# One fused hybrid decoder layer: the order of each engine's instructions made with the scheduler's detailed model of queues and semaphores

## The chip, the cores and the metric

The kernel runs on one core of one Trainium2 chip. A core has a matmul engine (TensorE, PE in the profile, with its weight loads as PEld), VectorE (DVE), ScalarE (ACT), GpSimd (POOL, nearly unused here) and SyncE (SP), which only issues DMAs here. Each engine takes its instructions in the order of its own queue and waits at an instruction until the semaphores it names have come. The metric is the device time of one execution in microseconds; the figure for a kernel is the median of three runs.

## The reference

One layer of a decoder trunk on a sequence of 2048 tokens with 1024 features, in float32. Three token mixers read the same normalised input through one projection, their outputs are joined and projected back, and a gated term is added:

```python
def hybrid_layer(x, p_i, pre_norm_w, w_in, ...):
    hn = rms_norm(x, pre_norm_w)
    u = jnp.einsum('bld,de->ble', hn, w_in)
    z, xbc, dt_raw, conf_in, conf_gate, q, k, v, attn_gate = split_columns(u)
    y_ssd = ssd_mixer(z, xbc, dt_raw, ssd_conv_w, ssd_conv_b, ...)
    y_conf = conformer_conv(conf_in, conf_dw_w, conf_dw_b, ...) * jax.nn.silu(conf_gate)
    y_attn = sliding_window_attention(q, k, v, attn_sinks, rel_bias) * jax.nn.silu(attn_gate)
    y = jnp.concatenate([y_ssd, y_conf, y_attn], axis=-1)
    h = x + rms_norm(jnp.einsum('ble,ed->bld', y, w_out), post_norm_w)
    gate = jax.nn.sigmoid(jnp.einsum('bld,de->ble', h, ple_gate))
    return h + jnp.einsum('blp,pd->bld', p_i, ple_proj) * gate
```

`ssd_mixer` is a state-space mixer with 16 heads in chunks of 128 tokens: within a chunk a masked product, between chunks a state that each chunk updates. `conformer_conv` is a causal convolution over 31 taps with a layer norm. `sliding_window_attention` has 8 heads on 2 key heads and looks back 128 tokens. `depth` is 1.

## The kernel before

The sequence is cut into four chunks of 512 tokens. Every large product is made of three matmuls on operands that are split into a high and a low part: hi·lo, lo·hi and hi·hi. `split` makes the parts, the high one on ACT (L190) and the low one on DVE (L191). A matmul of this kind has 512 columns; the projection has 4032 of them (L443, L444, L445), the output projection 1536 (L1048 to L1050), and the gate stage the rest (L207 to L209). They are the bulk of PE's work.

**Stage 1** makes the projection `w_in` and the three mixers, in two halves of two chunks. At the start chunk 0 is projected while the norm of its rows is still being made. For chunk 1 the order is fixed by data: `rsqrt_cols` (L142 to L151) gives rstd as columns, a transpose on PE (L175) turns them into a row, ACT copies it (L177) and writes it out by a DMA from its own queue (L179), SP loads it back to all partitions (L186), DVE weighs the chunk with it (L433, in `pre_apply`), and `split` gives the operands `ah` and `al`. The evictions of projected tiles (L478) multiply by such a row too (`rb__229` for chunk 0).

After the head a half runs through units: convolution (C), attention (A) and state-space (S) units, in turns. A unit's projection runs through `proj`, and the work behind it is written as generators that stand in the list `pending` and are advanced between groups of matmuls. An SSD unit (`ssd_front`, `ssd_back`) loads `Ab` (L868), transposes its input (L505), forms `xd` (L894) and `xw` (L896), `eA` and `Ab` by ACT (L899 to L904), makes state increments on PE (L910), carries the state `H` on DVE (L918), weighs `eA` and `Ab` on DVE (L927, L928), and multiplies into one PSUM tile `ps_y`: L937 from `Ab`, L940 from `eA` and `H`. A convolution of four taps is L487 on ACT, three L489 and an L492 on DVE. These small matmuls (64 or 128 columns wide, or the transposes) stand between the 512-column ones of the next unit's projection. Of the scratch tiles that hold 1024 columns (`Ab`, `eA`, the attention's `S`, and in stage 2 `ya`, `ysd`, `cvo`) there are four in all; PSUM has five tiles for projections (`ps_pp`), two for small products (`ps_m`) and one `ps_y`.

**Stage 2** multiplies by `w_out`, chunk by chunk. `prep` loads what the mixers wrote (L236: `ya`, `ysd`, `cvo`), norms and splits it. `stats` makes the norms for the next chunk, among them the column sums (L159) of `csum` (L263) and of `ssum`, and two rows through L175. **Stage 3** is the gated term.

The program is written with a tile framework. The kernel's text gives the tiles, the pools with their numbers of buffers, and a sequence of operations; the framework finds which operation needs which, plays the program on a model of the chip, and emits each engine's instructions in the order that the model gives. No priority is written by hand. The text of the kernel sets which work is offered at which time, the model sets what stands ahead of what on each queue, the SP queue and ACT's DMAs among them.

## Time and profile before

| | us |
|---|---|
| three runs | 1840.11, 1841.65, 1845.51 |
| median | 1841.65 |
| the profiled execution | 1850.51 |
| its span, first to last instruction | 1848.7 |
| DMA, mean over the span | 143 GB/s |

The profiled execution was 0.5% longer than the median. The profile's page lists busy time by engine, a chain of waits followed back from the last instruction, and groups of instructions by line. Two more views are used: the waits of one engine, with what they waited for, and stretches of the span with the busy time of each engine. A busy PE contains short gaps between matmuls, since their ends are modelled; distances between starts show those.

### The profile page before, as it was taken

How to read it: one execution, taken by the hardware profiler on the slowest of the kernel's cores; microseconds unless marked ns; L12 is line 12 of the kernel's file. 1: busy time of each engine (PE TensorE's matmuls, PEld its weight loads, DVE VectorE, ACT ScalarE, POOL GpSimd, SP SyncE). 2: the span in 40 equal slices, each digit the busy share in tenths (PEclk: the TensorE clock that was granted, in tenths of full speed). 3: DMA queues.
4: the chain of work that ended last, by engine and by line, in shares of the span. 5: the costliest groups of instructions: out<-in, count | busy, mean ns of one | idle time of the engine just before them, and what ended most of it. 6: DMA issues, size and time to landing. Idle time of an engine off the chain costs nothing.

```text
span 1848.7 us, 25168 instructions
## 1 busy us (share of the span) xinstructions
PE 1810.7 (98%) x9386; PEld 1461.6 (79%) x9386; DVE 1385.1 (75%) x2400; ACT 818.6 (44%) x1565; POOL 0.2 (0%) x4
## 2 busy tenths in 40 slices
PE   6999999999999999999999999999999999999998
PEld 5877787787888778878788887877888788887887
DVE  6859769759869875976975996988777867466543
ACT  5525425524726542542653371465444444343331
POOL 0000000000000000000000000000000000000000
PEclk9999999999999999999999999999999999999999
DMA  7443233224433433333332332346677766578554
GB/s 234 132 133 98 80 102 96 61 78 106 171 112 111 121 102 104 91 87 89 100 115 76 101 99 87 82 145 230 214 242 236 245 228 199 202 240 280 189 188 131
DMA packets 118982, 265.09 MB, mean 143 GB/s; under 512 B 12619, under 2 KB 20428, under 8 KB 118860
## 3 DMA queue, kind: packets, MB, share of 16 engines
q1 hardware_dynamic: 108428, 246.65, 40.9%
q10 hardware_dynamic: 10432, 16.83, 4.1%
q8 instruction: 74, 1.21, 0.3%
q14 instruction: 48, 0.39, 0.1%
HBM read 205.05 MB, written 39.50 MB: 132 GB/s over the span
## 4 chain that ended last, share of the span: by engine, by line
PE 78%; DMA 8%; DVE 6%; ACT 4%; issue 2%; ACTq 1%; SPq 0%; DVEq 0%
PE ps_pp L443 15%; PE ps_pp L444 14%; PE ps_pp L445 14%; PE ps_pp L1048 4%; PE ps_pp L1049 4%; PE ps_pp L1050 4%; PE ps_pp L208 3%; PE ps_pp L209 3%; PE ps_pp L207 3%; PE ps_m L766 2%; PE ps_y L940 2%; PE ps_y L838 2%; DMA Ab<-acs_d 2%; PE ps_y L937 2%; PE ps_m L816 1%
## 5 line engine op out<-in xcount | busy, mean ns | idle before, releaser
L443 PE MATMUL ps_pp<-al,whi 128*128 128x512 f32 x1344 | 536.6, 400 | 13.6 <-DVE al L393 10.4
L444 PE MATMUL ps_pp<-ah,wlo 128*128 128x512 f32 x1344 | 534.5, 398 | 0.0
L445 PE MATMUL ps_pp<-ah,whi 128*128 128x512 f32 x1344 | 534.1, 397 | 0.0
L191 DVE TENSOR_TENSOR wlo<-wst,whi 128x1024 fp32r<-128x1024 f32 x214 | 234.1, 1102 | 179.8 <-ACT whi L190 179.4
L443 PEld LDWEIGHTS ps_pp<-al,whi 128*128 128x128 f32 x1344 | 254.4, 189 | 73.1 <-DVE al L393 10.4
L190 ACT CAST whi<-wst 128x1024 fp32r<-128x1024 f32 x214 | 202.9, 951 | 242.0 <-DMA wst<-in_w_gate_dram 86.1
L691 DVE SCALAR_TENSOR_TENSOR acc<-gl,par_sb,acc 128x1024 f32<-128x1024 f32 x240 | 307.3, 1280 | 2.3
L444 PEld LDWEIGHTS ps_pp<-ah,wlo 128*128 128x128 f32 x1344 | 254.6, 189 | 55.8 <-issue 6.5
L445 PEld LDWEIGHTS ps_pp<-ah,whi 128*128 128x128 f32 x1344 | 254.5, 189 | 54.4 <-issue 4.9
L489 DVE SCALAR_TENSOR_TENSOR cv<-raw,par_sb,cv 128x512 f32<-128x512 f32 x144 | 107.6, 747 | 22.7 <-ACT cv L487 22.0
L208 PE MATMUL ps_pp<-ah,wlo 128*128 128x512 f32 x256 | 100.2, 391 | 3.7 <-DVE wlo L191 3.7
L1048 PE MATMUL ps_pp<-bl,whi 128*128 128x512 f32 x256 | 101.5, 399 | 0.6 <-ACT whi L190 0.6
L1048 PE MATMUL ps_pp<-al,whi 128*128 128x512 f32 x256 | 100.4, 393 | 0.7 <-DVE al L191 0.7
L1049 PE MATMUL ps_pp<-bh,wlo 128*128 128x512 f32 x256 | 101.1, 395 | 0.0
L1050 PE MATMUL ps_pp<-bh,whi 128*128 128x512 f32 x256 | 100.7, 394 | 0.0
L207 PE MATMUL ps_pp<-al,whi 128*128 128x512 f32 x256 | 100.1, 391 | 0.6 <-ACT whi L190 0.5
L1049 PE MATMUL ps_pp<-ah,wlo 128*128 128x512 f32 x256 | 100.1, 391 | 0.0
L1050 PE MATMUL ps_pp<-ah,whi 128*128 128x512 f32 x256 | 100.0, 390 | 0.0
L209 PE MATMUL ps_pp<-ah,whi 128*128 128x512 f32 x256 | 99.7, 389 | 0.0
L796 ACT ACTIVATE S<-S,nm 128x256 f32<-128x256 f32 (+1 forms) x128 | 62.8, 492 | 80.0 <-DVE nm L782 74.6
L903 ACT ACTIVATE Ab<-Ab,acs 128x128 f32<-128x128 f32 x256 | 82.4, 391 | 0.4
L937 PE MATMUL ps_y<-Ab,xd 128*64 128x128 f32 x512 | 61.5, 282 | 2.0 <-issue 2.0
(235 smaller groups left out, 2592.1 us busy)
## 6 DMA issues: line engine op xcount, KB each, us to landing
wst<-in_w_in_dram SPq DMA_DIRECT2D x88, 512.0 KB, 3.5
wst<-in_w_out_dram SPq DMA_DIRECT2D x64, 512.0 KB, 5.1
Ab<-acs_d SPq DMA_DIRECT2D x64, 256.0 KB, 4.5
ysd<-y_d SPq DMA_DIRECT2D x32, 512.0 KB, 5.5
wst<-in_w_gate_dram SPq DMA_DIRECT2D x32, 512.0 KB, 3.5
gl<-in_xT_dram SPq DMA_DIRECT2D x16, 512.0 KB, 4.0
qh<-qh ACTq DMA_DIRECT2D x64, 128.0 KB, 2.4
ql<-ql ACTq DMA_DIRECT2D x64, 128.0 KB, 2.4
```

Of the source, the lines that this page charges most:

```text
L190: A.copy(hi, src)
L191: V.tensor_tensor(out=lo, in0=src, in1=hi.bitcast(F32), op=ALU.subtract)
L207: PE.matmul(out, lhsT=hi[:, k, :], rhs=al, start=start and k == 0, stop=False)
L208: PE.matmul(out, lhsT=lo[:, k, :], rhs=ah, start=False, stop=False)
L209: PE.matmul(out, lhsT=hi[:, k, :], rhs=ah, start=False, stop=stop and k == nk - 1)
L443: PE.matmul(o_, lhsT=hi[:, k, :], rhs=al, start=k == 0, stop=False)
L444: PE.matmul(o_, lhsT=lo[:, k, :], rhs=ah, start=False, stop=False)
L445: PE.matmul(o_, lhsT=hi[:, k, :], rhs=ah, start=False, stop=k == KD - 1)
L691: V.scalar_tensor_tensor(out=acc, in0=gl[:, k:k + 2 * TC], scalar=pc("ccw", j * 31 + k), in1=acc, op0=ALU.mult, op1=ALU.add)
L1048: PE.matmul(pj[dd], lhsT=hi[:, i, :], rhs=yl, start=first, stop=False)
L1049: PE.matmul(pj[dd], lhsT=lo[:, i, :], rhs=yh, start=False, stop=False)
L1050: PE.matmul(pj[dd], lhsT=hi[:, i, :], rhs=yh, start=False, stop=last)
```

## The change

One argument is added where the kernel is built. The kernel's own text, its tiles and its pools are the same.

```diff
-    with _tile.TileContext(nc) as tc:
+    with _tile.TileContext(nc, schedule_with_timeline_sim=True) as tc:
         hybrid_block_kernel(tc, *args)
```

With it the framework plays the program on a more detailed model, with queues and semaphores, when it makes the order. Every engine gets the same instructions as before. On PE an instruction moves 36 places on average, on DVE 21, on ACT 6 and on SP 3; the last quarter of the program, the gate stage, has the same order on PE and DVE. Three places follow.

ACT, near the start of the program: the two rows of rstd (L177, L179) of chunks 0 and 1, with the split of the keys (`kh`) and the first four-tap convolution (`raw`, `cv`) of chunk 0. Rows with + stand there now.

```order
+L190 CAST whi<-wst 128x1024 x2
+L177 COPY rt<-ps_m 4x128
+L179 DMA row<-rt 4x128
 L190 CAST kh<-ks 128x512
+L177 COPY rt<-ps_m 4x128
+L485 COPY halS<-raw 128x3
+L487 ACTIVATE cv<-raw,par_sb 128x512
+L179 DMA row<-rt 4x128
 L483 COPY raw<-halS 128x3
```

The second row's DMA now stands behind the copy `halS` and the activation `cv`, both of which read `raw`; before, both copies and both DMAs stood ahead of `kh`, each with a cast of weights behind it. On PE the two transposes L175 of these rows move from places 63 and 79 to places 84 and 109, and the first matmul on chunk 1 from place 117 to 119.

PE, at the end of stage 1, before: the SSD unit whose product is `ps_y_10626`, and behind it the projection `ps_pp_10699`, one of the last ones.

```order
L940 MATMUL ps_y_10626<-eA_10549,H_10593 64x128 x2
L937 MATMUL ps_y_10626<-Ab_10426,xd_10545 64x128 x2
L940 MATMUL ps_y_10626<-eA_10549,H_10593 64x128 x2
L937 MATMUL ps_y_10626<-Ab_10426,xd_10545 64x128 x2
L940 MATMUL ps_y_10626<-eA_10549,H_10593 64x128 x2
L443 MATMUL ps_pp_10699<-al_5600,whi_10562 128x512
L444 MATMUL ps_pp_10699<-ah_5599,wlo_10563 128x512
L445 MATMUL ps_pp_10699<-ah_5599,whi_10562 128x512
L443 MATMUL ps_pp_10699<-al_5608,whi_10562 128x512
L444 MATMUL ps_pp_10699<-ah_5607,wlo_10563 128x512
L445 MATMUL ps_pp_10699<-ah_5607,whi_10562 128x512
```

The same unit's end and what follows it now, down to the first matmul of the output projection:

```order
L940 MATMUL ps_y_10626<-eA_10549,H_10593 64x128 x2
L937 MATMUL ps_y_10626<-Ab_10426,xd_10545 64x128 x2
L940 MATMUL ps_y_10626<-eA_10549,H_10593 64x128
L505 MATMUL ps_m_10676<-cst_sb_77,cv_10618 128x128 x4
L940 MATMUL ps_y_10626<-eA_10549,H_10593 64x128
L937 MATMUL ps_y_10762<-Ab_10572,xd_10681 64x128 x2
L940 MATMUL ps_y_10762<-eA_10685,hcar_97 64x128 x2
L937 MATMUL ps_y_10762<-Ab_10572,xd_10681 64x128 x2
L910 MATMUL ps_m_10712<-xw_10683,Bn_8272 128x128 x4
L1048 MATMUL ps_pp_10951<-al_10729,whi_10955 128x512
L1049 MATMUL ps_pp_10951<-ah_10728,wlo_10956 128x512
L1050 MATMUL ps_pp_10951<-ah_10728,whi_10955 128x512
```

Before, wide matmuls stood between the units; now all of the projection stands ahead of the last three units (`ps_y_10490`, `ps_y_10626`, `ps_y_10762`), and these follow one another with no wide matmul between them until L1048.

DVE, in the last units of the first half, before: the state updates of one unit (`H_5141`) with the convolution `cv_5166` of the next.

```order
L489 SCALAR_TENSOR_TENSOR cv_5166<-raw_5162,par_sb_79,cv_5166 128x512
L918 SCALAR_TENSOR_TENSOR H_5141<-hcar_97,eat_182,ps_m_5136 128x64 x2
L918 SCALAR_TENSOR_TENSOR H_5141<-H_5141,eat_182,ps_m_5136 128x64 x4
L489 SCALAR_TENSOR_TENSOR cv_5166<-raw_5162,par_sb_79,cv_5166 128x512
L918 SCALAR_TENSOR_TENSOR hcar_97<-H_5141,eat_182,ps_m_5136 128x64
L489 SCALAR_TENSOR_TENSOR cv_5166<-raw_5162,par_sb_79,cv_5166 128x512
L918 SCALAR_TENSOR_TENSOR hcar_97<-H_5141,eat_182,ps_m_5136 128x64
L942 SCALAR_TENSOR_TENSOR cv_4981<-cv_4981,par_sb_79,ps_y_5174 128x512
L492 SCALAR_TENSOR_TENSOR cv_5166<-cth_5171,cv_5166 128x512
```

The same updates now:

```order
L918 SCALAR_TENSOR_TENSOR H_5141<-hcar_97,eat_182,ps_m_5136 128x64 x2
L191 TENSOR_TENSOR al_5616<-gl_5611,ah_5615 128x1024
L489 SCALAR_TENSOR_TENSOR cv_5166<-raw_5162,par_sb_79,cv_5166 128x512
L918 SCALAR_TENSOR_TENSOR H_5141<-H_5141,eat_182,ps_m_5136 128x64
L928 TENSOR_TENSOR Ab_5110<-Ab_5110,CBm_3003 128x1024
L918 SCALAR_TENSOR_TENSOR H_5141<-H_5141,eat_182,ps_m_5136 128x64
L489 SCALAR_TENSOR_TENSOR cv_5166<-raw_5162,par_sb_79,cv_5166 128x512
L918 SCALAR_TENSOR_TENSOR H_5141<-H_5141,eat_182,ps_m_5136 128x64 x2
L918 SCALAR_TENSOR_TENSOR hcar_97<-H_5141,eat_182,ps_m_5136 128x64 x2
L492 SCALAR_TENSOR_TENSOR cv_5166<-cth_5171,cv_5166 128x512
L942 SCALAR_TENSOR_TENSOR cv_4981<-cv_4981,par_sb_79,ps_y_5174 128x512
```

Between the updates there now stand the split of chunk 3 for the second half (`al_5616`) and the weighing L928 of the next unit's `Ab_5110`.

## The prediction

> **What bounds the kernel now.** The page of the profile comes first, its busy line and its chain, because they say which engine's order matters.
>
> ```profile
> PE 1810.7 (98%) x9386; PEld 1461.6 (79%) x9386; DVE 1385.1 (75%) x2400; ACT 818.6 (44%) x1565; POOL 0.2 (0%) x4
> ...
> PE 78%; DMA 8%; DVE 6%; ACT 4%; issue 2%; ACTq 1%; SPq 0%; DVEq 0%
> ```
>
> PE, the matmul engine, is the bound: it is busy in 98% of the span of 1848.7 us, and 78% of the chain that ended last is its own work. VectorE (DVE) has a quarter of the span free. An order can therefore win only what PE loses, in waits or in needless switches, and it can lose by making PE wait. The waits of PE are the second view.
>
> ```profile
> PE ps_pp L443 <- DVE al L393: 10.4, 1, 10.4
> ...
> PE ps_m L159 <- DVE csum L263: 3.6, 1, 3.6
> PE ps_y L940 <- DVE H L918: 3.5, 6, 1.2
> PE ps_pp L443 <- DVE al L191: 3.2, 1, 3.2
> ...
> PE ps_m L766 <- DMA ql<-ql: 1.2, 3, 0.5
> PE ps_m L159 <- DVE ssum L231: 1.0, 1, 1.0
> PE ps_m L607 <- DVE da L596: 1.0, 2, 0.5
> ```
>
> The columns are the sum, the count and the longest. The first 10.4 us are the start, which no order shown here shortens. The others shown are some 13 us, under 1% of the span. The third view, stretches of 50 us, places the losses at the borders between stages.
>
> ```profile
> 0.00:50.00 50.00, 35.89 (x140) 27.83 (x141) 32.32 (x70) 27.02 (x44) 0.20 (x4) 0.94 0.71 233
> 600.00:650.00 50.00, 47.80 (x288) 37.80 (x285) 43.94 (x76) 25.72 (x47) 0.00 (x0) 1.00 0.44 129
> 650.00:700.00 50.00, 48.70 (x250) 38.50 (x248) 35.15 (x64) 23.05 (x45) 0.00 (x0) 1.00 0.29 92
> 1200.00:1250.00 50.00, 48.84 (x309) 37.47 (x305) 42.35 (x81) 33.34 (x69) 0.00 (x0) 1.00 0.40 137
> 1250.00:1300.00 50.00, 49.41 (x253) 40.28 (x252) 42.16 (x52) 26.06 (x30) 0.00 (x0) 1.00 0.70 236
> 1450.00:1500.00 50.00, 46.37 (x210) 38.18 (x209) 35.83 (x57) 20.42 (x25) 0.00 (x0) 0.97 0.70 244
> ```
>
> After the length come the busy times of PE, weight loads, DVE, ACT and POOL, then the granted PE clock. PE misses 14.1 us in the first stretch, 2.2 and 1.3 around the change from the first half of stage 1 to the second, 1.2 and 0.6 around its end, and 3.6 in stage 2.
>
> Two prices inside a busy PE are needed as well. The timeline gives both.
>
> ```profile
> 1204.91 0.39 PE L445 MATMUL ps_pp<-ah,whi 128*128 128x512 f32 x1
> 1205.14 0.39 PE L443 MATMUL ps_pp<-al,whi 128*128 128x512 f32 x1
> ...
> 1206.39 0.48 PE L445 MATMUL ps_pp<-ah,whi 128*128 128x512 f32 x1
> 1206.70 0.40 PE L443 MATMUL ps_pp<-al,whi 128*128 128x512 f32 x1
> ...
> 1473.67 1.12 PE L159 MATMUL ps_m<-ones,csum 128*128 128x2 f32 x8 [3.63 <-DVE csum L263]
> ...
> 1475.23 0.63 PE L1049 MATMUL ps_pp<-bh,wlo 128*128 128x512 f32 x1
> 1475.66 0.63 PE L1050 MATMUL ps_pp<-bh,whi 128*128 128x512 f32 x1
> ```
>
> A 512-column matmul starts 0.23 us after the one before it (1204.91 to 1205.14; over many rows 0.227). Behind a group of small ones the first takes 0.31 (1206.39 to 1206.70), so each group costs some 0.08 besides its own work. After the idle 3.63 us the distance is 0.43 (1475.23 to 1475.66), 0.2 too much; this lasts some 14 matmuls, so a long hole costs about 2.9 us more than itself.
>
> **The change part by part.** Nothing is added or removed: the same instructions stand on every queue, in another order. Each term is what PE loses more (+) or less (−).
>
> *Start.* The row of rstd values of chunk 1 is made by a transpose (L175), a copy, a DMA from ACT's queue (L179) and a broadcast load from SP (L186); behind it DVE weighs chunk 1 (L433) and splits it, and PE starts on chunk 1. The first line is the view of the tile `row`, the others are the timeline.
>
> ```profile
> DMA to landing us min/median/max: 3.3/3.3/3.3
> ...
> 28.81 0.27 PE L175 MATMUL ps_m<-cst_sb,cols 128*4 128x128 f32 x1
> ...
> 31.53 0.34 SPq L186 DMA_DIRECT2D rb__229<-row  x1
> ...
> 32.96 0.27 PE L175 MATMUL ps_m<-cst_sb,cols 128*4 128x128 f32 x1 [0.43 <-DVE cols L151]
> ...
> 33.55 0.25 ACTq L179 DMA_DIRECT2D row<-rt  x1
> ...
> 34.71 1.11 SPq L186 DMA_DIRECT2D acc<-row  x1
> ...
> 36.07 0.68 DVE L478 TENSOR_TENSOR ks<-ps_pp,rb__229 128x512 f32<-128x512 f32 x1
> ...
> 41.14 2.74 DVE L433 SCALAR_TENSOR_TENSOR gl<-gl,par_sb,acc 128x512 f32<-128x512 f32 x4 [2.41 <-DMA acc<-row]
> ...
> 43.80 1.22 DVE L191 TENSOR_TENSOR al<-gl,ah 128x1024 fp32r<-128x1024 f32 x1
> ...
> 44.86 0.82 ACT L487 ACTIVATE cv<-raw,par_sb 128x512 f32<-128x512 f32 x1
> ...
> 45.07 0.79 PE L443 MATMUL ps_pp<-al,whi 128*128 128x512 f32 x1 [3.19 <-DVE al L191]
> ```
>
> In the new PE order the first transpose stands 21 places later and the second 30 places later, nearly all 512-column matmuls: 28.8 becomes 33.6, and 33.0 becomes 39.8. The first row is loaded 2.7 us behind its transpose (28.81 to 31.53) and lands 3.3 us on, so at 39.6. ACT's queue, in the rows shown under the change, now holds the second row's DMA behind the copy L485 and the activation L487, which need `raw`, evicted by DVE with the first row. Two evictions at 0.6 us each give 41.0, L487 0.8 and the copy 0.2 give 42.1, the load goes out 1.2 later (33.55 to 34.71) and lands 6.4 later (34.71 to 41.14), at 49.7. Then 3.9 us to the end of the first `al` (41.14 to 45.02), and 1.4 for an L492 and an L489 that now stand between: 55.0 in place of 45.1. PE has the same work ahead of that point, so the loss is 9.9. I take **+9**, since the waits that follow close behind can forgive a little; bounds +7 (the 30 places alone count) and +11.
>
> *Interior of stage 1.* In the new order a small matmul stands some twenty 512-column matmuls (about 4.5 us) behind the one it depends on, where before it often came just in time; the waits L940 3.5, L766 1.2 and L607 1.0 have this cause, together 5.7. The groups of small matmuls between wide ones fall from 290 to 228: 62 × 0.08 = 5.0. With 1 for waits too short for the list, **−12**; bounds −19 (the unlisted restarts go too) and +3 (each later operand meets a busy DVE).
>
> *Change of half.* The new DVE order weighs chunks 2 and 3 (L433, then L191) ahead of and inside the last state updates of the first half, as the third place under the change shows, so PE's L940 wait there. The two windows lose 3.5 us now and should lose about as much: **0**, bounds −4 and +5.
>
> *End of stage 1.* Of the new PE order the last 512-column matmul of the projection comes before the last three SSD units, which follow as one lump of small matmuls; then the output projection begins.
>
> ```profile
> 1218.28 0.60 PE L505 MATMUL ps_m<-cst_sb,cv 128*128 128x128 f32 x4
> ...
> 1224.97 0.48 PE L940 MATMUL ps_y<-eA,H 128*64 128x128 f32 x3
> ...
> 1226.00 0.44 PE L940 MATMUL ps_y<-eA,H 128*64 128x128 f32 x3
> ...
> 1227.20 0.37 SPq L236 DMA_DIRECT2D ya<-y_d  x1
> ...
> 1234.77 1.23 DVE L191 TENSOR_TENSOR al<-ya,ah 128x1024 fp32r<-128x1024 f32 x1 [2.02 <-ACT ah L190]
> ```
>
> The first operand of the output projection, `ya`, is loaded into a buffer that the unit y_10626 releases with its last L940 (ended 1226.4). From there to the end of `al` are 9.6 us. Before, wide matmuls filled them; now PE has about 2 us of small ones: a hole of 7.6. Inside the lump the unit itself needs 6.7 us from its transpose to its first L940 with a new state (1218.28 to 1224.97), of which PE fills some 3: 3.7 more. The restart at the lower clock adds 2.9. Less the 1.8 that the two windows lose now this is 12.4; I take **+12**, bounds +5 (the hole stays short of the slow clock, and the unit's chain is hidden) and +16 (the last unit's chain is in line too).
>
> The Trainium skill's "Perfetto Trace Analysis" (Optimization Strategy) advises interleaving the stages of a kernel that load different engines. Before, this border did so and lost 1.8 us by the rows above; by that rule the new order, which parts the stages, is the worse one, and if only the lump were put back the sum would be −7 and not +5. The skill's "TensorE: Matmul & The Clock Gate" (HAM oscillation) lets the clock fall only after an idle of more than about 3.4 us; if the lump's holes were each shorter, the term would by it be 9 and not 12. The row at 1473.67 agrees, with 3.63 us.
>
> *Stage 2.* The column sums L159 now stand further behind their operands: 3.6 and 1.0 of wait and 2.9 of slow clock, −7.5 at most. But the transpose that gives the next chunk's row stands some 20 matmuls later in the chunk, and what hangs on it has little cover: up to 4 back. **−4**, bounds −8 and +4.
>
> *Gate stage.* The order is the same: **0**.
>
> The sum is 9 − 12 + 0 + 12 − 4 + 0 = +5 us. The profiled execution took 1850.5 us, so the same one would take 1855.5; the runs' median is 1841.65, and there the sum gives 1846.7.
>
> **The rivals.**
>
> *The interior pays more.* A busy PE hides short restarts, which the waits do not list. If all go (−19), stage 2 keeps its gain (−7.5), the change of half gains 4, and the end of stage 1 costs +5 with the start at +9: 9 − 19 − 4 + 5 − 7.5 = −16.5, or 1825. For it speaks that PE's listed waits are a small part of what the restarts can hide; against it that it needs every bound at its good end.
>
> *The state updates come late.* This is the slower side. In the new order DVE's six L918 of a unit are split up by longer work, and in five of 32 units by L928 of the next unit, which waits for a load of `Ab`. Between L910 and the L940 that need H, PE has 23 wide matmuls, 5.2 us. One line of the page's groups and one of the timeline price the chain.
>
> ```profile
> L489 DVE SCALAR_TENSOR_TENSOR cv<-raw,par_sb,cv 128x512 f32<-128x512 f32 x144 | 107.6, 747 | 22.7 <-ACT cv L487 22.0
> ...
> 1224.99 0.85 DVE L918 SCALAR_TENSOR_TENSOR H<-H,eat,ps_m 128x64 f32<-128x64 f32 x4
> ```
>
> Two L489 (0.75 each), an L191 (1.2 in the start's rows) and six updates (0.21 each) take 4.0 us; an L928, as long as an L191 of the same shape, makes 5.2, all that PE has. From there each wait of L928 for `Ab` is PE's too: at 0.7 us in 32 units +22, so +27, or 1869. Against it: only five units hold an L928 inside.
>
> *The order does nothing.* If queues wait on the same events the time is 1841.65. The orders differ in nearly every row of stage 1, so little speaks for it.
>
> **How the numbers follow.** A measurement of this kernel can tell 0.3%, 5.5 us, from no change. The forecast has 0.50; its own range is −5 to +14 (1837 to 1856), with 0.26 inside 5.5 us and 0.24 above. The interior's gain has 0.25: 0.22 faster, 0.03 within. The late updates have 0.22, all slower. No effect has 0.03. So faster 0.22, same 0.32, slower 0.46. The range goes from 1827 to 1868: it takes in all of the forecast, most of the first rival and most of the second, and leaves some 0.1 on each side.
>
> **What would show it.** The start is right if PE's wait for the `al` of chunk 1 (now 3.2 us) grows beyond 10 and the first L443 on it begins near 55 us. The interior is right if PE's waits for H (L940), `ql` and `da` add up to less than 2 us and the stretches from 75 to 590 us are about 6 us shorter in all. The end of stage 1 is right if a hole of some 7 us stands ahead of the first L1048 and 1200 to 1250 shows the clock below 1.00. Stage 2 is right if L159's 3.6 is gone. A wait for H in many units proves the second rival; a start at 45 us, or a border without a hole, proves the terms +9 or +12 wrong, and the time then falls below 1840.

## The result and the profile after

The changed kernel takes 1904.28 us (median of four runs, 1902.18 to 1906.64) against 1842.76 us for the kernel before (median of four, 1840.11 to 1845.51). The ratio is 1.0334, with a 95% interval of 1.0312 to 1.0356: it is slower. The forecast was 1846.7 us, and the time lies outside the range of 1827 to 1868. The profiled execution of the changed kernel took 1902.57 us, 52.1 more than that of before (1850.51). The points below are made between these two executions.

One figure of the section on the change is wrong: on DVE an instruction moves 8 places on average and not 21, because rows of one line had been paired by numbers that the two builds don't share.

The busy line and the chain of the page of the changed kernel:

```profile
PE 1818.5 (96%) x9386; PEld 1477.4 (78%) x9386; DVE 1394.2 (73%) x2400; ACT 818.5 (43%) x1565; POOL 0.2 (0%) x4
...
PE 74%; DMA 12%; DVE 8%; ACT 4%; issue 2%; SPq 0%; ACTq 0%; DVEq 0%
```

The busy times hardly differ from before. In the chain that ended last, PE's own share falls from 78% to 74%, and DMA, DVE and ACT rise from 18% to 24%: PE is still the bound, but more of the end is set by work that it waits for. The waits of PE (sum, count, longest) say for what:

```profile
PE ps_m L505 <- DVE cv L492: 16.6, 10, 6.2
PE ps_y L940 <- DVE H L918: 11.4, 11, 2.7
PE ps_pp L443 <- DVE al L393: 9.3, 1, 9.3
PE ps_pp L1048 <- DVE al L191: 6.5, 2, 4.7
PE ps_m L159 <- DVE ssum L231: 6.1, 1, 6.1
PE ps_y L937 <- issue: 5.8, 2, 4.4
PE ps_y L838 <- ACT pT L823: 3.4, 1, 3.4
...
PE ps_pp L443 <- DVE al L191: 0.7, 1, 0.7
```

All waits of the list add up to 76.8 us, against 32.8 before. The 9.3 us of the start is as it was (10.4). New or grown are the first two rows, both small matmuls that wait for DVE (the second from 3.5), the waits of the output projection's first operand (6.5, from 0.7), of a column sum (6.1, from 1.0), of an L937 (5.8, from 2.0), and of an attention product (3.4). The granted clock adds to it: its mean falls from 0.994 to 0.979. The stretches of 50 us (length, busy time of PE, weight loads, DVE, ACT and POOL, granted clock, DMA share, GB/s):

```profile
0.00:50.00 50.00, 32.71 (x138) 25.79 (x139) 33.95 (x73) 28.76 (x49) 0.20 (x4) 0.94 0.62 217
600.00:650.00 50.00, 42.97 (x243) 34.20 (x238) 44.07 (x86) 29.20 (x62) 0.00 (x0) 0.91 0.47 145
650.00:700.00 50.00, 47.22 (x286) 36.94 (x286) 33.64 (x66) 25.86 (x53) 0.00 (x0) 0.95 0.21 59
1200.00:1250.00 50.00, 50.00 (x280) 41.39 (x279) 39.28 (x80) 25.98 (x68) 0.00 (x0) 1.00 0.27 85
1250.00:1300.00 50.00, 33.92 (x222) 26.60 (x221) 38.73 (x69) 24.03 (x44) 0.00 (x0) 0.86 0.38 121
1450.00:1500.00 50.00, 41.14 (x173) 33.38 (x172) 35.81 (x61) 21.90 (x26) 0.00 (x0) 0.86 0.70 241
```

PE now misses 7.0 and 2.8 us around the change of half (2.2 and 1.3 before), 16.1 around the end of stage 1, which now lies behind 1250, and 8.9 in the one of stage 2 (3.6 before). In four of the six the clock is at 0.95 or less where it was 0.97 to 1.00.

**Where the time went.** At a handful of places both orders have issued exactly the same set of matmuls. The start of the next matmul there, in the one trace and in the other, gives the loss of each stretch:

| stretch, by the trace of before (us) | forecast | measured |
|---|---|---|
| start, 0 to 127 | +9 | +2.9 |
| interior of stage 1, 127 to 536 and 667 to 1147 | −12 | +12.4 (6.2 and 6.2) |
| change of half, 536 to 667 | 0 | +11.9 |
| end of stage 1, 1147 to 1317 | +12 | +17.9 |
| stage 2, 1317 to 1591 | −4 | +7.0 |
| gate stage, 1591 to the end | 0 | −0.1 |
| sum | +5 | +52.0 |

The medians differ by 61.5, since the profiled execution of before was some 8 us above its median and that of the changed kernel 2 below. Within a stretch the loss swings: compared at equal numbers of 512-column matmuls (times by the trace of before) the changed kernel is up to 13 us ahead (at 226 us) and then 11 behind (at 265), 11 ahead at 632 and 21 behind at 666. It pulls wide matmuls forward, puts the small ones off, and pays them back in lumps.

Two things make up the 52 us. PE's listed waits are 44.0 us longer. And the granted clock is at half for 80 us in all, against 25 before; there the wide matmuls start some 0.43 us apart and not 0.23, which costs 22.0 us over the whole timeline against 8.6, so 13 more. What is left, some −5, is about what the prediction gave to the smaller number of groups (288 before, 226 now), but no run measures that by itself. In the interior of stage 1 the waits grow by 10.8 us (5.2 to 16.0), and the slow clock costs 5.3 more. Of these 5.3, 2.9 lie right behind the cut at 127 us and behind a wait of 1.6 us that counts to the start, so the start and the interior could as well be put at 5.9 and 9.4.

The change of half shows how. This is PE's timeline (start, length, instruction; the brackets hold the idle time before it and what ended it):

```profile
636.69 0.39 PE L937 MATMUL ps_y<-Ab,xd 128*64 128x128 f32 x4
639.73 0.52 PE L940 MATMUL ps_y<-eA,H 128*64 128x128 f32 x3 [2.66 <-DVE H L918]
...
641.91 0.69 PE L940 MATMUL ps_y<-eA,H 128*64 128x128 f32 x2 [1.33 <-DVE H L918]
643.24 0.48 PE L940 MATMUL ps_y<-eA,H 128*64 128x128 f32 x1 [0.64 <-DVE H L918]
...
647.57 0.63 PE L469 MATMUL ps_pp<-al,whi 128*128 128x512 f32 x1
647.99 0.63 PE L470 MATMUL ps_pp<-ah,wlo 128*128 128x512 f32 x1
...
651.75 0.40 PE L469 MATMUL ps_pp<-al,whi 128*128 128x512 f32 x1
651.99 0.40 PE L470 MATMUL ps_pp<-ah,wlo 128*128 128x512 f32 x1
...
657.52 0.63 PE L505 MATMUL ps_m<-cst_sb,cv 128*128 128x128 f32 x4 [2.78 <-DVE cv L492]
```

And this is DVE's over the same time:

```profile
638.75 0.74 DVE L489 SCALAR_TENSOR_TENSOR cv<-raw,par_sb,cv 128x512 f32<-128x512 f32 x1
639.41 0.46 DVE L918 SCALAR_TENSOR_TENSOR H<-hcar,eat,ps_m 128x64 f32<-128x64 f32 x2
639.79 1.22 DVE L191 TENSOR_TENSOR al<-gl,ah 128x1024 fp32r<-128x1024 f32 x1
640.93 0.74 DVE L489 SCALAR_TENSOR_TENSOR cv<-raw,par_sb,cv 128x512 f32<-128x512 f32 x1
641.59 0.27 DVE L918 SCALAR_TENSOR_TENSOR H<-H,eat,ps_m 128x64 f32<-128x64 f32 x1
641.78 1.21 DVE L928 TENSOR_TENSOR Ab<-Ab,CBm 128x1024 f32<-128x1024 f32 x1
642.91 0.27 DVE L918 SCALAR_TENSOR_TENSOR H<-H,eat,ps_m 128x64 f32<-128x64 f32 x1
643.11 0.74 DVE L489 SCALAR_TENSOR_TENSOR cv<-raw,par_sb,cv 128x512 f32<-128x512 f32 x1
```

Each L940 of PE waits for the next update L918, and between two updates stand an L191 of the second half, an L928 of the next unit, and an L489: 1.2, 0.7 and 1.2 us of other work for 0.2 us of update. The three waits are 4.6 us. Behind them the clock is at half: two wide matmuls stand 0.42 us apart (647.57 to 647.99), and 0.24 again at 651.75.

### The profile page after: what moved, and what is told of

Read it like the earlier page. It is cut to its first block, busy times and chain, and to the rows that moved or that the text cites. A ratio compares the mean times of both kernels' runs of the same rounds, so it can differ in the third digit from the quotient of the medians.

```text
span 1900.8 us, 25176 instructions
## 1 busy us (share of the span) xinstructions
PE 1818.5 (96%) x9386; PEld 1477.4 (78%) x9386; DVE 1394.2 (73%) x2400; ACT 818.5 (43%) x1565; POOL 0.2 (0%) x4
## 4 chain that ended last, share of the span: by engine, by line
PE 74%; DMA 12%; DVE 8%; ACT 4%; issue 2%; SPq 0%; ACTq 0%; DVEq 0%
PE ps_pp L443 15%; PE ps_pp L444 15%; PE ps_pp L445 15%; PE ps_pp L1048 3%; PE ps_pp L1049 3%; PE ps_pp L1050 3%; PE ps_pp L208 3%; PE ps_pp L209 3%; PE ps_pp L207 3%; PE ps_m L766 2%; PE ps_y L940 2%; DMA Ab<-acs_d 1%; PE ps_y L838 1%; PE ps_y L937 1%; DMA h_d<-xres 1%
## 5 line engine op out<-in xcount | busy, mean ns | idle before, releaser
L191 DVE TENSOR_TENSOR wlo<-wst,whi 128x1024 fp32r<-128x1024 f32 x214 | 234.7, 1101 | 165.0 <-ACT whi L190 164.4
L443 PEld LDWEIGHTS ps_pp<-al,whi 128*128 128x128 f32 x1344 | 256.1, 191 | 72.4 <-DVE al L393 9.3
L489 DVE SCALAR_TENSOR_TENSOR cv<-raw,par_sb,cv 128x512 f32<-128x512 f32 x144 | 107.7, 748 | 8.5 <-ACT cv L487 6.5
L1048 PE MATMUL ps_pp<-al,whi 128*128 128x512 f32 x256 | 102.7, 403 | 6.6 <-DVE al L191 6.5
L1048 PE MATMUL ps_pp<-bl,whi 128*128 128x512 f32 x256 | 100.1, 392 | 1.4 <-issue 1.4
L491 ACT ACTIVATE cth<-cv 128x512 f32<-128x512 f32 x48 | 30.2, 629 | 123.1 <-DVE cv L489 123.1
L927 DVE TENSOR_TENSOR eA<-eA,CT 128x1024 f32<-128x1024 f32 x32 | 39.1, 1223 | 47.3 <-ACT eA L899 47.3
```

What stands on the lines that cost most here:

```text
L191: V.tensor_tensor(out=lo, in0=src, in1=hi.bitcast(F32), op=ALU.subtract)
L443: PE.matmul(o_, lhsT=hi[:, k, :], rhs=al, start=k == 0, stop=False)
L1048: PE.matmul(pj[dd], lhsT=hi[:, i, :], rhs=yl, start=first, stop=False)
```

## The experiments

Three numbers are used beside the times. They are medians over the whole trace, worked out from the timelines: **lag**, from the end of a DVE operand to the start of the small matmul on PE that needs it; **H chain**, from the end of L910 to the last update L918 of H; and **softmax tail**, from the end of the attention's exponential on ACT to the end of the L805 that PE's L816 reads. The waits are the sum of PE's list, the clock is the mean.

| kernel | us | ratio (95%) | waits | clock | lag | H chain | softmax tail |
|---|---|---|---|---|---|---|---|
| before | 1842.76 | | 32.8 | 0.994 | 0.64 | 1.77 | 3.14 |
| after | 1904.28 | 1.0334 (1.0312 to 1.0356) | 76.8 | 0.979 | 3.93 | 4.37 | 5.73 |
| e1_pe_before | 2047.35 | 1.1098 (1.1037 to 1.1159) | 169.9 | 0.966 | 0.66 | 3.74 | 7.38 |
| e2_dve_act_before | 2038.32 | 1.1049 (1.0984 to 1.1114) | 174.1 | 0.962 | 3.45 | 1.28 | 3.14 |
| e3_pe_after | 1937.19 | 1.0501 (1.0444 to 1.0558) | 101.9 | 0.971 | 4.36 | 1.74 | 2.45 |
| e4_dve_act_after | 1944.21 | 1.0539 (1.0478 to 1.06) | 93.0 | 0.977 | 0.77 | 5.92 | 5.46 |
| e5_late4 | 1878.8 | 1.0191 (1.0147 to 1.0236) | 58.5 | 0.993 | 1.49 | 2.21 | 3.33 |
| e6_late7 | 1902.73 | 1.0321 (1.0257 to 1.0386) | 72.4 | 0.982 | 1.71 | 2.00 | 3.46 |
| e9_same8 | 1887.1 | 1.0235 (1.0192 to 1.0277) | 62.2 | 0.988 | 1.24 | 1.74 | 3.40 |
| e10_early4 | 1914.71 | 1.0385 (1.0341 to 1.0429) | 89.0 | 0.978 | 4.28 | 1.53 | 2.02 |
| e13_ahead32 | 2036.33 | 1.1079 (1.1024 to 1.1135) | 174.7 | 0.955 | 3.01 | 3.38 | 6.75 |
| e16_queue16 | 1899.16 | 1.0312 (1.0282 to 1.0342) | 70.4 | 0.984 | 3.09 | 3.76 | 6.45 |
| e17_queue8 | 1934.19 | 1.0503 (1.0448 to 1.0557) | 80.5 | 0.976 | 2.18 | 4.55 | 7.63 |
| e18_queue4 | 1975.55 | 1.0727 (1.0696 to 1.0758) | 91.8 | 0.970 | 1.55 | 4.48 | 7.99 |

Each ratio is against the kernel before as it ran in the same batch. Only the order of the instructions differs between these kernels, and in one, further below, the buffers. Kernels that are not in the table have their ratios with them in the text.

### Which engine's order

The program is built twice: once for its order on some engines, then again with these engines held to that order (an edge without a semaphore from each instruction to the next), and the rest of the order made anew by the one model or the other.

```diff
+            for names in (pin or {}).values():
+                names = [n for n in names if n in traced]
+                for u, v in zip(names, names[1:]):
+                    tc.add_manual_dep(traced[v], u, _mybir.DependencyInfo(_mybir.DependencyClass.NoSync, _mybir.DependencyReason.DATA), reason="order")
...
+    SIM = {"schedule_with_timeline_sim": True}
+    nc, arrays = build(order(build()[0], E.PE), **SIM)
```

This is the first of four, with PE's order of before in the changed kernel. In the second DVE and ACT are held to their order of before. The other two are the kernel before with PE's order of after, and with DVE's and ACT's.

> The detailed model makes the order, but PE is held to the order it had before; DVE, ACT and SP are free. Theory P (the loss lies in PE's own order: matmuls put where their operands are not there yet, and small ones in lumps without cover): 1840 to 1855. Theory V (the loss lies in the orders of DVE and ACT: long work ahead of short chains): 1875 to 1905, since those are still made by the detailed model.

> The detailed model makes the order, but DVE and ACT are held to the orders they had before; PE and SP are free. Theory P: 1885 to 1905. Theory V: 1840 to 1860.

> The simple model makes the order, but PE is held to the order of the changed kernel; DVE, ACT and SP are free. Theory P: 1885 to 1905, the whole loss. Theory V: 1845 to 1870.

> The simple model makes the order, but DVE and ACT are held to the orders of the changed kernel; PE and SP are free. Theory P: 1845 to 1870. Theory V: 1885 to 1905, the whole loss.

They came out at 2047.35, 2038.32, 1937.19 and 1944.21 us, all four slower than both whole kernels, which neither theory had forecast. Mixing costs more than the change itself, so these runs can't say how the change's loss divides between the engines. The waits of PE in the first of them:

```profile
PE ps_m L816 <- DVE S L805: 41.6, 14, 5.1
PE ps_y L940 <- DVE H L918: 33.7, 37, 2.2
```

With PE's order of before, a small matmul comes as early as it did before, but DVE's results, ordered by the detailed model around it, come late (H chain 3.74, softmax tail 7.38): 37 matmuls wait for H. In the kernel before with PE's order of after it is the reverse: the chains are short (1.74 and 2.45), the results lie waiting (lag 4.36), and PE's longest waits are transposes whose convolution was ordered later:

```profile
PE ps_m L505 <- DVE cv L492: 33.7, 10, 10.4
```

The orders that one model makes together fit one another; an engine held to the other model's order breaks the fit.

### Small matmuls later, on their own

The kernel before, with PE held to its order of before, but each dependent small matmul moved 4 or 7 wide matmuls later for each step that its chain on PE has (the others moved as little as keeps their order among themselves). If that alone made the loss, the time should climb towards 1904.

```diff
+    STEP = {505: 1, 910: 2, 937: 3, 940: 3, 766: 1, 816: 2, 838: 3, 159: 1, 175: 2, 530: 1, 607: 2, 608: 2, 615: 3}
...
+                        at = max(at, wides + n * STEP.get(line, 0))
...
+    nc, arrays = build(later(build()[0], 4))
```

> The simple model makes the order of DVE, ACT and SP; PE keeps the order it had before, but each dependent small matmul stands 4 wide matmuls (0.9 us) later per step of its chain (state-space unit: transpose 4, increments 8, products 12). The changed kernel has 3.3 us per step into PE. Theory L (the loss is this lag: chains of small work take longer, and where wide work runs out PE waits): 1850 to 1868. Rival R (the lag only gives slack, the loss lies elsewhere in the order): 1832 to 1848.

> As the run with 4, with 7 wide matmuls (1.6 us) per step. Theory L: 1863 to 1888, about half of the loss of the changed kernel and clearly above the run with 4. Rival R: 1832 to 1850.

The times were 1878.8 and 1902.73 us, both above what theory L gave: to put the small matmuls off costs as much as the whole change, although DVE's chains stay short (2.2 and 2.0). But the loss lies elsewhere. By the stretches of the table the second run loses some 30 us in the interior of stage 1 (12.4 with the change), some 5 at the change of half (11.9), and nothing in stage 2 (7.0). So the equal total doesn't show that the change's loss is this one. A uniform delay was to say whether the growing distance from step to step is needed for that. Every dependent small matmul moves 8 wide ones later, the same for all:

```diff
-                        at = max(at, wides + n * STEP.get(line, 0))
+                        at = max(at, wides + n * (line in STEP))
...
+    nc, arrays = build(later(build()[0], 8))
```

> Control for the runs with 4 and 7: PE's order of before with every dependent small matmul 8 wide matmuls (1.8 us) later, the same for each step, so that a chain starts later and has more slack at its first step, but its later steps are no further apart. Theory L (each step of a chain grows by the lag): clearly below the run with 4, 1843 to 1862. Rival M (any shift of PE's order against the others costs): 1880 to 1905, by the size of the shift.

1887.1 us: a uniform delay costs 44 us too, as rival M had it, so the growing distance isn't needed. The reverse was tried on PE's order of after in the kernel before (1937.19 unmoved, e3 above): each small matmul 4 or 8 wide ones earlier for each step.

> PE's order of the changed kernel, held, with each dependent small matmul 4 wide matmuls (0.9 us) earlier per step; DVE, ACT and SP by the simple model. With PE's order unmoved this gave 1937. Theory L: 1900 to 1920. Rival M: 1935 to 1980.

> As the run with 4 earlier, with 8 (1.8 us) per step, somewhat over half of the lag of 3.3 us. Theory L: 1870 to 1900, below the run with 4. Rival M: 1950 or more.

The first gives 1914.71 us, 22 less than unmoved; the second 1941.78 us (1.0531, 1.0487 to 1.0575), no better than unmoved and in neither range. So with DVE, ACT and SP ordered by the simple model the small matmuls can stand too late and too early. This speaks for a lag that is too long, but not for lag as the only cause.

### The buffer at the end of stage 1

In the prediction the hole at the end of stage 1 began with the buffer that `ya` shares with the last units. Here `ya` has a buffer of its own, paid for with one of the two `rt`, in the changed kernel.

```diff
-        rt = wk.tile([n, P], F32, tag="rt", name="rt", bufs=2)
+        rt = wk.tile([n, P], F32, tag="rt", name="rt", bufs=1)
...
-        t = pair(t1024(name))
+        t = pair(wk.tile([P, 2 * TC], F32, tag="ya", name=name, bufs=1) if name == "ya" else t1024(name))
```

> The changed kernel's option, with a buffer of its own for the first operands of the output projection (ya), so that its load need not wait for a state-space unit to release one; one buffer fewer for rt makes room. If the hole at the end of stage 1 is the wait for this buffer, as the prediction's step said: 1882 to 1896, and no wait of some 5 us of the first L1048 on al. If the hole only moves into the last units, whose chains have no cover: 1898 to 1906.

It took 1899.14 us (1.0302, 1.0256 to 1.0347), 5 less than the changed kernel, with the two intervals overlapping. The wait of L1048 for `al` fell from 6.5 to 0.2 us, but PE's list has two rows that grew (L940 from 11.4, and a wait of L1048 that is new):

```profile
PE ps_y L940 <- DVE H L918: 19.0, 12, 4.5
...
PE ps_pp L1048 <- DVE bl L191: 7.8, 4, 3.2
```

Of the first row's growth 6 us lie at this border (8.9 us there against 2.7 in the changed kernel); the second row's waits lie in stage 2. The shared buffer makes the wait for `al`, but without it the next chain of the border ends last: by the stretches of the table the end of stage 1 costs 17.8 us here and 17.9 with the shared buffer. So the buffer isn't what this border's loss comes from.

### Which stretches

The two whole orders can be spliced at places where every engine has issued the same set. The first splice is after's order but for 1004 to 1312 us (the end of stage 1), which is before's. The second is before's order, with after's in the two stretches in which the changed kernel gains, 255 to 412 and 682 to 1004 us (places by the trace of before).

```diff
+                pin[e][u:v] = other[e][u:v]
...
+    nc, arrays = build(spliced(simple, detailed, ('start', 1004), (1312, 'end')))
```

> All four engines held: the changed kernel's order from the start to 1004 us (of the time before) and from 1312 us on, the order of before in between, where the changed kernel loses 29 us more. If the loss belongs to the order of the stretch itself: 1870 to 1880. If it is handed on from stretch to stretch (buffers held, engines behind): 1890 to 1905.

> All four engines held: the order of before, but in the two inner stretches 255 to 412 us and 682 to 1004 us, where the changed kernel gained 2 and 4 us on the one before, the changed kernel's order. If a stretch's order carries its own gain: 1835 to 1839, ratio 0.995 to 0.998. If the gain is only borrowed (small work put off to the next stretch): 1842 to 1850.

The first took 1876.0 us (1.0176, 1.0137 to 1.0215), 28 less than the changed kernel. Compared at the places 1004 and 1312 in the same way as in the table, the changed kernel loses 29 us between them (it is 15.8 us behind at the first and 45.1 at the second), and this splice 3.2: the loss goes with the order of that stretch. The second took 1844.29 us, a ratio of 1.0007 (0.9986 to 1.0027). After's order gained 2 and 4 us in those two stretches of its own trace; in the splice they gain nothing that the time shows. Its trace tells why for the second: the two stretches do gain 2.1 and 2.4 us on the trace of before, but 3.6 us are lost again between 1004 and 1147, where the order is before's. Right behind the cut PE waits 2.1 us for two column sums (L159), of which the trace of before lists none there, and the granted clock is 0.85 from 997 to 1020 (0.93 before). So that gain was borrowed, although every engine has issued the same set at the cut; what became of the first one can't be told from one trace. Neither splice beats the kernel before.

### How far PE may run ahead

The last theory was that the detailed model lets wide matmuls run ahead in PE's queue and so makes the lag. Two ways to bound this were tried. In the first a matmul can be placed only behind the one that stands 32, 64 or 128 before it in the order of the program's text:

```diff
+            for u, v in zip(pe, pe[near:]) if near else ():
+                tc.add_manual_dep(v, u.name, _mybir.DependencyInfo(_mybir.DependencyClass.NoSync, _mybir.DependencyReason.DATA), reason="near")
...
+    nc, arrays = build(order(build(near=32, **SIM)[0], *ALL))
```

> The detailed model makes the order of all engines, but while it does so a matmul counts as ready only behind the one 32 before it on PE; then all four engines are held to that order. Theory L (PE's running ahead in the model is the cause): 1835 to 1855, median distance from DVE's result to the small matmul below 1.5 us. Rival R (the rest of the detailed model): 1885 to 1910.

> As the run with 32, with 64. Theory L: 1838 to 1865. Rival R: 1885 to 1910.

> As the run with 32, with 128, a limit that the model rarely meets. Theory L: between, 1865 to 1900, above the runs with 32 and 64. Rival R: 1885 to 1910, no difference between the three.

2036.33, 2028.61 (1.1037, 1.0983 to 1.1092) and 1964.87 us (1.0691, 1.066 to 1.0722), all above every range given. The row of PE's list that is new in the first shows what it did:

```profile
PE ps_m L816 <- DVE S L805: 79.2, 16, 8.5
```

The bound is counted in the text's order, so it pushes late small matmuls ahead of their operands. It isn't a bound on a queue and settles nothing on the lag. The second way bounds the lead itself while the order is made: a mark on POOL follows every 8 (4, 2) wide matmuls, and a wide matmul must wait for the mark before the last one, so that PE's lead is at most some 16 (8, 4) of them. All engines of a kernel without the marks are then held to that one order, so that they fit one another.

```diff
+            if len(self.mark) > 1:
+                self.tc.add_manual_dep(r.ins, self.mark[-2], dep, reason="pace")
...
+    nc, arrays, _ = build(pin=build(pace=8, schedule_with_timeline_sim=True)[2])
```

> The detailed model makes one order for all engines, with at most 16 wide matmuls (3.6 us) in PE's queue in the model. Theory L (small matmuls stand late because the model's PE queue is already full of wide ones): 1870 to 1900, and the median distance from DVE's result to the small matmul between 2.0 and 3.9 us. Rival R (the rest of the detailed model): 1895 to 1960.

> As the run before, with at most 8 wide matmuls (1.8 us). Theory L: 1850 to 1880, distance 1.2 to 2.2 us. Rival R: 1895 to 1960.

> As the run before, with at most 4 wide matmuls (0.9 us). Theory L: 1838 to 1862, distance about 1 us. Rival R: 1895 to 1960.

1899.16, 1934.19 and 1975.55 us. The lag falls as intended, from 3.93 to 3.09, 2.18 and 1.55 us; the time stays as it is with the first, where both ranges held 1899, and rises with the others, against theory L. DVE's chains don't become shorter: the H chain is at 3.8 to 4.6 us, the softmax tail at 6.5 to 8.0. PE's list of the last one:

```profile
PE ps_m L766 <- DMA qh<-qh: 14.9, 5, 3.2
PE ps_y L940 <- DVE H L918: 11.5, 16, 2.8
...
PE ps_m L910 <- DVE xw L896: 7.4, 7, 2.0
```

With the same late results PE now stands ahead of them more often. So the theory falls: in the detailed model's orders the lag isn't only a cost, it is also what hides results that come late.

## Why the prediction was wrong, point by point

**Interior of stage 1: the step that failed.** It said that a small matmul some twenty wide ones later no longer waits, took 5.7 us of waits and 5.0 of groups as won, and gave −12. Measured is +12.4. The number of groups did fall (288 to 226), but the step set PE's new order against the times at which operands came before, as if only PE's order were new. The operands come later too: the H chain grew from 1.77 to 4.37 us, with other DVE work inside it up from 0.67 to 2.84, the softmax tail from 3.14 to 5.73, and L487 to L492 of a convolution from 6.42 to 7.63. The waits that were to go (L940, L766 and L607, 5.7 over the whole kernel) did not: the sign named for this step was under 2 us for H, `ql` and `da`, and H alone makes 11.4, with 16.6 for L505. In the interior itself all listed waits grow from 5.2 to 16.0 us (5.3 for L505, 4.0 for L940, 3.4 for an L838), and the slow clock, which the step left out, adds 5.3. The first experiment shows the same from the other side: with PE's early order and these chains, 33.7 us are lost on H alone. The bound of +3, "each later operand meets a busy DVE", was the right mechanism, but too small. The second splice shows that the parts of the interior that looked like a gain bring none to the whole.

**The second rival was the right mechanism, at too small a chance and too narrow a place.** It had DVE's updates split up by longer work and PE waiting for H, at 0.22 and 1869 us. A unit late in the second half shows it as it was priced; DVE's rows:

```profile
1131.44 0.75 DVE L489 SCALAR_TENSOR_TENSOR cv<-raw,par_sb,cv 128x512 f32<-128x512 f32 x1
1132.10 0.47 DVE L918 SCALAR_TENSOR_TENSOR H<-H,eat,ps_m 128x64 f32<-128x64 f32 x2
1132.48 0.75 DVE L489 SCALAR_TENSOR_TENSOR cv<-raw,par_sb,cv 128x512 f32<-128x512 f32 x1
1133.15 1.22 DVE L928 TENSOR_TENSOR Ab<-Ab,CBm 128x1024 f32<-128x1024 f32 x1
1134.28 0.47 DVE L918 SCALAR_TENSOR_TENSOR H<-H,eat,ps_m 128x64 f32<-128x64 f32 x2
```

PE's L940 then waits 1.34 us at 1134.61. What the rival left out is that the convolution and the softmax have the same trouble, and that a wait need not be in every unit: the 11 waits for H and 7 of the 10 for `cv` come in four clusters, two at borders (640 to 658 and 1256 to 1272 us) and two inside stage 1 (240 to 243 and 1132 to 1147), and with each the clock falls to half.

**Two readings in the working were off too.** A long hole was priced at 2.9 us for some 14 slow matmuls; behind the hole at 1473.67 the timeline has eight slow distances (1474.66 to 1478.10), 1.6 us more than at the full clock. And between a unit's L910 and the L940 that need H the new order has a median of 15 wide matmuls to the first of them and 17.5 to the last, 3.4 to 4.0 us and not 23 and 5.2: the second rival counted on more cover than there was.

**Change of half: mis-sized, +11.9 for 0 (bounds −4 and +5).** The place was named and its rows of DVE were shown, but their price was set to "about as much as now". The rows above have 4.6 us of waits for H, some twenty wide matmuls at about 0.2 us too much (12 behind 641 us and 8 behind 658), and the 2.78 us of an L505 for `cv` at 657.52.

**End of stage 1: right in the place and the lump, wrong in the buffer, +17.9 for +12 (bounds +5 and +16).** PE's rows:

```profile
1265.79 0.70 PE L937 MATMUL ps_y<-Ab,xd 128*64 128x128 f32 x4 [4.45 <-issue]
...
1270.63 0.52 PE L940 MATMUL ps_y<-eA,H 128*64 128x128 f32 x3 [1.29 <-DVE H L918]
...
1281.14 0.80 PE L1048 MATMUL ps_pp<-al,whi 128*128 128x512 f32 x1 [4.70 <-DVE al L191]
```

The hole of "some 7 us" ahead of the first L1048 is there with 4.70, since the last unit's small matmuls filled more of it, and a second one of 4.45 stands inside the lump. Part of the lump runs with the clock at half (1262.6 to 1269.4 us, and again from 1279.7, where the first L1048 takes 0.80 and not 0.39). The Trainium skill's "Perfetto Trace Analysis" (Optimization Strategy), which advises interleaving regimes with different limits, fits what was seen: the parted border cost 17.9 us more than the interleaved one, though the orders of DVE and ACT changed there too. The buffer's release, taken as the cause of the hole, is only the last of several chains there: with a buffer of its own for `ya` the border costs 17.8.

**Start: right direction by luck, +2.9 for +9, since the wait took another form.** PE and ACT:

```profile
36.51 0.27 PE L175 MATMUL ps_m<-cst_sb,cols 128*4 128x128 f32 x1
...
37.80 0.25 ACT L177 COPY rt<-ps_m 4x128 f32<-4x128 f32 x1
38.05 0.81 ACT L487 ACTIVATE cv<-raw,par_sb 128x512 f32<-128x512 f32 x1
38.08 0.26 ACTq L179 DMA_DIRECT2D row<-rt  x1
...
46.75 1.12 PE L505 MATMUL ps_m<-cst_sb,cv 128*128 128x128 f32 x4 [6.16 <-DVE cv L492]
...
48.54 0.80 PE L443 MATMUL ps_pp<-al,whi 128*128 128x512 f32 x1 [0.68 <-DVE al L191]
```

The transpose came at 36.5 and not at 39.8, because PE waited less ahead of it. The second row's DMA went out at 38.08 while L487, which stands ahead of it in ACT's queue, still ran to 38.86: it needs only the copy's result, and the step had let it wait for the activation's end (42.1). So PE reached chunk 1 at 48.5 and not at 55.0 (45.1 before). The wait moved: PE stands 6.16 us at an L505 whose `cv` was put behind four L433 on DVE, and the `al` is all but ready then (a wait of 0.68, where more than 10 was forecast).

**Stage 2: +7.0 for −4.** The wait of 3.6 for `csum` is gone, as the step had it, but it counted only what goes. In its place stands a chain that was hidden: a row's DMA, `cvo`, its square on ACT, an L228 and two L231 on DVE, and the column sum:

```profile
1480.98 0.68 DVE L231 TENSOR_TENSOR ssum<-ssum,sq 128x512 f32<-128x512 f32 x1
...
1481.81 0.34 PE L159 MATMUL ps_m<-ones,ssum 128*128 128x2 f32 x1 [6.14 <-DVE ssum L231]
```

**Gate stage: right**, −0.1 for 0.

**What is shown and what stays open.** Shown: the loss of the end of stage 1 goes with the order of that stretch (the first splice), orders of the two models do not mix (the first four), small matmuls that are put off cost tens of microseconds where the simple model orders the other engines (e5, e6, e9), and a shorter lead of PE does not cure the detailed model's order (e16 is as slow as the changed kernel, e17 and e18 are slower). Only argued: that it is the split of DVE's and ACT's chains that makes the detailed model's orders slower. For it speaks that each kernel of the table whose DVE order comes from the detailed model has a softmax tail of 5.5 to 8.0 us and an H chain of 3.4 to 5.9, while with the simple model's DVE orders these are 2.0 to 3.5 and 1.3 to 2.2. Against a full account stands e2, which has these two chains short (its convolutions take 10.2 us) and is among the slowest. A run in which only these chains are shortened within one consistent order was not tried, and neither was one that finds which part of the model makes them so.

## What to carry to other kernels

The orders of the engines belong together: the slack that a later place on one engine seems to win must be held against when its operands will come in the new order of the others, not in the old trace. Where a scheduler puts off small dependent work, look at the borders between stages, where no wide work is left to hide it; in a profile, compare the times at which both kernels have done the same set of matmuls, and look past the end of a stretch that gains, since the gain may be paid back there. A wait that is removed should be priced together with the chain that ends next.

## What the runs showed of the hardware that was not expected

The slow clock came without one long hole. At the change of half the longest idle of PE is 2.66 us, followed by 1.33 and 0.64 within seven microseconds with little work between, and the wide matmuls behind stand 0.42 us apart up to 651; the granted clock is 0.50 from 641.4 to 651.6 and 0.91 in the stretch of 50 us. The prediction had weighed only single holes beyond some 3 us. The Trainium skill's "TensorE: Matmul & The Clock Gate" (A second HAM failure mode: psum-queue depth-cycling) tells of frequent short idles that take the clock down; these rows agree.

The clock also fell with no idle listed at all. In the kernel before, PE worked from 1004.43 to 1007.15 us on column sums alone (L159, two columns wide, 24 rows of the trace) without a wait, and the granted clock is 0.50 from 1006.9 to 1010.3, with wide matmuls 0.43 us apart. So a lump of small matmuls can go with the slow clock by itself; which of them do was not tried.

A DMA issue in ACT's queue did not wait for the end of the activation ahead of it: 38.08 us, 0.03 us behind the start of an L487 of 0.81 us.
